# Seven products instead of eight for half of the row pairs of a 256x8192x2048 product in fp32, with its stationaries sent to DRAM and read back

## The chip, the cores and the metric

The kernel runs on one core of a Trainium2 chip. The metric is device time in microseconds (us) of one execution; lower is better. Engines are named as in the profile: PE is the matrix engine (PEld its weight loads), DVE, ACT and POOL are the vector, scalar and general engines, SP issues most of the DMAs.

## The reference, cut to what matters

One encoder layer on 256 tokens of 2048 features: a mixer of two attention branches, then a squared-ReLU MLP. The change touches only the MLP, and in it the down projection:

```python
h = rms_norm(x, norm_mlp_pre)
u = square(relu(h @ w_up))           # [256, 2048] @ [2048, 8192]
x = x + rms_norm(u @ w_down, norm_mlp_post)   # [256, 8192] @ [8192, 2048], all fp32
```

## The kernel before

Every fp32 product is made of parts. A weight block of 1 MB is loaded by SP into a `raw` buffer (`load`, L98), ACT casts it into `hi` (L115), DVE subtracts to get `lo` (L116). `raw`, `hi` and `lo` have three buffers each (pool `wp`, `bufs=3`), so SP's load of block n+3 waits until DVE's subtraction of block n has freed the `raw` buffer. SP works through its DMAs in order: what stands behind a waiting load waits too.

Up projection (the loop over 16 groups `cg` of 512 columns, 4 weight blocks each): weights are stationary, the transposed normalised input is moving (`wgroup`, L191 and L192). Each of a group's four banks `u_p` is taken out by ACT (`up_r`, L254), DVE (`up_s`, L256 and L761) and ACT (`u`, L762). The 16 results `u` [128, 4, 256] stay in SBUF as pages, transposed: 512 rows of the down projection by 256 tokens.

Down projection (L769 to L819): activations are stationary, `w_down` is moving. `usplit` (L746, L747) makes the parts `uh`, `ul` of a group of four 128-row blocks. A step k takes one block of 128 rows and all 2048 columns: two token tiles `t`, four column blocks `c` of 512, and for each of these eight accumulators `acc` three matmuls of 128x128 by 128x512 (L777, L778, L779: `uh` with `hi`, `uh` with `lo`, `ul` with `hi`), 24 a step, 64 steps, 1536 in all. The eight accumulators fill all eight PSUM banks. The last three steps (`LAST = 3`) go accumulator by accumulator, token tile 0 first, so that most of the evacuation runs under the products that are left. Evacuation of an accumulator is a square with a sum on ACT (`jd`, L807) and a multiplication by the gain on DVE (`zw`, L809). Per token tile then follow the mean and the inverse root (`sd`, `rd`, L811 and L85 on DVE, L88 on POOL), four times scale-and-add of the residual on DVE (L816), and four stores (L819).

The program order on every engine is set when the program is built, by a list scheduler with a cost model; code order only breaks ties, except where `issue_after` pins an instruction. On the chip each engine takes its instructions in that order.

## Time and profile before

| | |
|---|---|
| three runs | 1395.98, 1396.07, 1398.43 us, median 1396.07 us |
| profiled execution | span 1394.5 us; its own device time is not given apart, the median lies 1.6 us above the span |
| PE busy | 1374.6 us (99%) |
| DVE, ACT, POOL busy | 835.8 us (60%), 668.7 us (48%), 7.9 us (1%) |
| DMA | 265.16 MB, mean 190 GB/s |

The profile page gives the busy time of each engine over the whole span and in 40 slices, the DMA queues, the chain of work that ended last, and the costliest groups of instructions. An engine counts as busy while it has an instruction in work; matmuls overlap, so the time between the starts of two of them is shorter than the 389 ns that one is given. The first step of a reading is which engine the chain runs through, and the second whether the others have room in the stage that is changed.

### The profile page before, as it was taken

To read this page: it belongs to the slowest core of one execution; us is meant where nothing else is said; L and a number is where in the kernel's file an instruction comes from. 1 tells how busy PE (TensorE), PEld (TensorE's weight loads), DVE (VectorE), ACT (ScalarE), POOL (GpSimd) and SP (SyncE) were. 2 spreads that over 40 slices of the span, in tenths; PEclk is the share of its full clock that TensorE was granted. 3 is DMA by queue.
4 is the path that set the end of the run, shared out by engine and by line. 5 is a ranking of instruction groups with operands and counts; after the bars stand their busy time and mean duration, and the time that the engine had idled before them with its cause. 6 is when DMAs were issued, how large, how long until landed. Compare 5 with 4: busy or idle time off the path is not lost.

```text
span 1394.5 us, 17896 instructions
## 1 busy us (share of the span) xinstructions
PE 1374.6 (99%) x7240; PEld 1177.8 (84%) x7240; DVE 835.8 (60%) x1155; ACT 668.7 (48%) x1023; POOL 7.9 (1%) x19
## 2 busy tenths in 40 slices
PE   7999999999999999999899999999999999999997
PEld 6888888888888888888788888888888888888886
DVE  6868866676656565654755555555575554444445
ACT  7554554545444445543744444444464543334332
POOL 0000000000000000000000000000000000000000
PEclk9999999999999999999999999999999999999999
DMA  9674755564555555675455565656555556555551
GB/s 317 202 214 154 202 177 173 171 191 155 165 205 182 203 181 183 203 279 184 149 182 181 182 193 170 211 170 200 189 196 185 203 186 227 195 187 205 181 199 73
DMA packets 117490, 265.16 MB, mean 190 GB/s; under 512 B 15008, under 2 KB 16288, under 8 KB 109216
## 3 DMA queue, kind: packets, MB, share of 16 engines
q1 hardware_dynamic: 117264, 264.03, 57.3%
q8 instruction: 56, 0.92, 0.3%
q14 instruction: 26, 0.21, 0.0%
q10 hardware_dynamic: 144, 0.01, 0.0%
HBM read 261.92 MB, written 3.92 MB: 191 GB/s over the span
## 4 chain that ended last, share of the span: by engine, by line
PE 98%; DVE 1%; DMA 0%; ACT 0%; SPq 0%; issue 0%; DVEq 0%; POOLq 0%; POOL 0%; ACTq 0%
PE u_p L191 17%; PE u_p L192 9%; PE acc L779 8%; PE acc L778 8%; PE acc L777 8%; PE gb_p L191 4%; PE ga_p L191 4%; PE qa_p L191 2%; PE gb_p L192 2%; PE ga_p L192 2%; PE ka_p L191 2%; PE qn_p L191 2%; PE bb_p L191 2%; PE ba_p L191 2%; PE kn_p L191 2%; PE y_p L229 2%
## 5 line engine op out<-in xcount | busy, mean ns | idle before, releaser
L191 PE MATMUL u_p<-h2T,u_h 128*128 128x512 f32 x1024 | 359.9, 398 | 0.5 <-DVE r_m L85 0.5
L192 PE MATMUL u_p<-h2T,u_l 128*128 128x256 f32 x1024 | 284.3, 280 | 0.0
L116 DVE TENSOR_TENSOR d_l<-d_w,d_h 128x1024 fp32r<-128x1024 f32 x128 | 151.1, 1221 | 164.2 <-ACT d_h L115 163.7
L116 DVE TENSOR_TENSOR u_l<-u_w,u_h 128x1024 fp32r<-128x1024 f32 x128 | 151.1, 1222 | 146.0 <-ACT u_h L115 144.7
L191 PEld LDWEIGHTS u_p<-h2T,u_h 128*128 128x128 f32 x1024 | 192.0, 189 | 45.5 <-DVE r_m L85 0.9
L115 ACT CAST d_h<-d_w 128x1024 fp32r<-128x1024 f32 x128 | 128.3, 1052 | 191.1 <-PE acc L779 187.5
L778 PE MATMUL acc<-d_l,uh 128*128 128x512 f32 x512 | 199.0, 389 | 0.0
L779 PE MATMUL acc<-d_h,ul 128*128 128x512 f32 x512 | 198.9, 389 | 0.0
L777 PE MATMUL acc<-d_h,uh 128*128 128x512 f32 x512 | 198.2, 389 | 0.0
L192 PEld LDWEIGHTS u_p<-h2T,u_l 128*128 128x128 f32 x1024 | 193.8, 189 | 1.3
L115 ACT CAST u_h<-u_w 128x1024 fp32r<-128x1024 f32 x128 | 128.0, 1049 | 123.9 <-PE u_p L191 62.5
L778 PEld LDWEIGHTS acc<-d_l,uh 128*128 128x128 f32 x512 | 96.1, 188 | 20.1
L777 PEld LDWEIGHTS acc<-d_h,uh 128*128 128x128 f32 x512 | 96.1, 188 | 20.0
L779 PEld LDWEIGHTS acc<-d_h,ul 128*128 128x128 f32 x512 | 96.1, 188 | 19.8
L191 PE MATMUL gb_p<-hT,gb_h 128*128 128x512 f32 x256 | 90.4, 398 | 0.0
L191 PE MATMUL ga_p<-hT,ga_h 128*128 128x512 f32 x256 | 90.0, 397 | 0.0
L192 PE MATMUL gb_p<-hT,gb_l 128*128 128x256 f32 x256 | 71.4, 281 | 0.0
L192 PE MATMUL ga_p<-hT,ga_l 128*128 128x256 f32 x256 | 70.3, 280 | 0.0
L191 PEld LDWEIGHTS gb_p<-hT,gb_h 128*128 128x128 f32 x256 | 47.9, 188 | 11.5
L116 DVE TENSOR_TENSOR gb_l<-gb_w,gb_h 128x1024 fp32r<-128x1024 f32 x32 | 37.8, 1221 | 31.1 <-ACT gb_h L115 31.1
L191 PEld LDWEIGHTS ga_p<-hT,ga_h 128*128 128x128 f32 x256 | 47.4, 188 | 10.5
L116 DVE TENSOR_TENSOR y_l<-y_w,y_h 128x1024 fp32r<-128x1024 f32 x32 | 37.9, 1222 | 27.8 <-ACT y_h L115 27.8
(213 smaller groups left out, 2348.1 us busy)
## 6 DMA issues: line engine op xcount, KB each, us to landing
u_w<-in_w_up SPq DMA_DIRECT2D x64, 1024.0 KB, 5.4
d_w<-in_w_down SPq DMA_DIRECT2D x64, 1024.0 KB, 4.9
ga_w<-in_w_in SPq DMA_DIRECT2D x16, 1024.0 KB, 5.2
gb_w<-in_w_in SPq DMA_DIRECT2D x16, 1024.0 KB, 5.2
y_w<-in_w_out SPq DMA_DIRECT2D x16, 1024.0 KB, 5.1
ka_w<-in_w_in SPq DMA_DIRECT2D x8, 1024.0 KB, 6.1
va_w<-in_w_in SPq DMA_DIRECT2D x8, 1024.0 KB, 5.2
qn_w<-in_w_in SPq DMA_DIRECT2D x8, 1024.0 KB, 5.1
```

Source lines behind the costliest of these rows:

```text
L115: nc.scalar.copy(hi[part], raw[part])
L116: nc.vector.tensor_sub(lo[part], raw[part], hi[part].bitcast(F32))
L191: nc.tensor.matmul(ps[b], hi[:, k % 4, cs], mv, start=(k == 0), stop=False)
L192: nc.tensor.matmul(ps[b][:, :T], lo[:, k % 4, cs], mv[:, :T], start=False, stop=(k == nk - 1))
L229: nc.tensor.matmul(ps[t], sh, hi[:, k % 4], start=(k == 0), stop=False)
L777: nc.tensor.matmul(acc[t][c], uh[:, k % 4, ts_], hi[:, 0, cs], start=(k == 0), stop=False)
L778: nc.tensor.matmul(acc[t][c], uh[:, k % 4, ts_], lo[:, 0, cs], start=False, stop=False)
L779: nc.tensor.matmul(acc[t][c], ul[:, k % 4, ts_], hi[:, 0, cs], start=False, stop=(k == NK - 1))
```

## The change

A step of the new down projection takes two blocks of 128 rows (a row pair) and half of the columns (1024, `g` = 0 or 1), again 1 MB of `w_down`. It is a product of 2x2 blocks: two token tiles by two row blocks, two row blocks by two column blocks of 512. For odd groups `cg` ("eight") it is done as before, eight block products, 24 matmuls. For even ones ("seven") it is done with seven products of sums of blocks, 21 matmuls: four sums of activation blocks are made once (`sums`, on DVE), four sums of weight blocks in each step (`dt`, on DVE), and the products are put together from eight banks `p{g}0` to `p{g}7` when all row pairs of the half are summed (`zw`, on DVE). There are 32 steps of either kind; the matmuls go from 1536 to 1440.

All steps of `g = 0` come before those of `g = 1`, so each stationary is used twice, in times far apart. Stationaries are made behind each group of the up projection (`act_sets`: `ah`, `al`), written to DRAM by POOL (`keep`), and read back by SP, for each `g` anew (`act_again`: `bh`, `bl`), two groups ahead of their use. The pool `tmp` is closed behind the up projection, and its room goes to the parts `eh`, `el` of the weight sums, with one buffer each. `dr`, `dh`, `dl` are the weight block as loaded and its two parts, with three buffers each as before.

```diff
+    temps = ctx.enter_context(ExitStack())
+    tmp = temps.enter_context(tc.tile_pool(name="tmp", bufs=6))
...
+    NG = DFF // 512
+    kept = {}
+    def seven_of(cg):
+        return cg % 2 == 0
+    def act_sets(cg, u):
+        srcs = []
+        if seven_of(cg):
+            a11, a21 = u[:, 0:2, :P], u[:, 0:2, P:]
+            a12, a22 = u[:, 2:4, :P], u[:, 2:4, P:]
+            sums = page([P, 4, 2, P], F32, f"sm{cg}")
+            nc.vector.tensor_sub(sums[:, 0], a21, a22)
+            nc.vector.tensor_sub(sums[:, 1], a11, a21)
+            nc.vector.tensor_sub(sums[:, 2], sums[:, 0], a11)
+            nc.vector.tensor_add(sums[:, 3], a12, sums[:, 2])
+            srcs = [
+                ([P, 3, 2, P], [(slice(0, 1), u[:, 0:2, :P].unsqueeze(1)),
+                                (slice(1, 3), u[:, 2:4].rearrange("p k (t q) -> p t k q", t=2))]),
+                ([P, 4, 2, P], [(slice(0, 4), sums)]),
+            ]
+        else:
+            srcs = [([P, 4, T], [(slice(0, 4), u)])]
+        for i, (shape, pieces) in enumerate(srcs):
+            hi, lo = page(shape, F32R, f"ah{cg}{i}"), page(shape, F32R, f"al{cg}{i}")
+            for at, src in pieces:
+                nc.scalar.copy(hi[:, at], src)
+                nc.vector.tensor_sub(lo[:, at], src, hi[:, at].bitcast(F32))
+            for n, part in (("h", hi), ("l", lo)):
+                kd = dram.tile(shape, F32, name=f"keep{n}{cg}{i}", tag=f"keep{n}{cg}{i}")
+                nc.gpsimd.dma_start(kd, part.bitcast(F32))
+                kept[cg, i, n] = (shape, kd)
+    def act_again(cg, g):
+        out = []
+        for i in range(2 if seven_of(cg) else 1):
+            got = []
+            for n in "hl":
+                shape, kd = kept[cg, i, n]
+                t = page(shape, F32R, f"b{n}{g}{cg}{i}")
+                nc.sync.dma_start(t.bitcast(F32), kd)
+                got.append(t)
+            out.append(got)
+        return out
+    for cg in range(NG):
         u = page([P, 4, T], F32, f"u{cg}")
 
         def u_evac(b, ps, u=u):
@@ -762,57 +799,139 @@
             nc.scalar.activation(u[:, b], s, AF.Square)
 
         wgroup(a["w_up"], cg * 512, lambda k: hT2[k // 2][:, k % 2], KD, u_evac, f"u{cg}", **({} if cg else first_up))
-        uT.append(u)
-        if cg == DFF // 512 - 2:
-            usplit(0)
-
...
+        act_sets(cg, u)
+    temps.close()
+    down = ctx.enter_context(tc.tile_pool(name="down", bufs=1, reuse_waits="tile"))
+    wd = a["w_down"].rearrange("(g h j p) c -> p h g j c", h=2, j=2, p=P)
+    def wtile(tag, name):
+        return wp.tile([P, 4, 512], F32R, tag=tag, name=name)
+    def down_weights(g, cg, j):
+        raw = wp.tile([P, 4, 512], F32, tag="raw", name=f"dr{g}{cg}{j}")
+        last_load[0] = nc.sync.dma_start(
+            raw.rearrange("p (h b) c -> p h (b c)", h=2),
+            wd[:, :, cg, j, g * 1024 : (g + 1) * 1024],
+        ).ins
+        n = f"{g}{cg}{j}"
+        h1, l1 = wtile("hi", f"dh{n}"), wtile("lo", f"dl{n}")
+        if not seven_of(cg):
+            nc.scalar.copy(h1, raw)
+            nc.vector.tensor_sub(l1, raw, h1.bitcast(F32))
+            return h1, l1
+        t = [page([P, 2, 512], F32, f"dt{n}{i}") for i in range(2)]
+        nc.scalar.copy(h1[:, 1:4], raw[:, 1:4])
+        nc.vector.tensor_add(t[0], raw[:, 1:3], raw[:, 0:1].to_broadcast([P, 2, 512]))
+        nc.vector.tensor_add(t[1][:, 0], t[0][:, 0], raw[:, 2])
+        nc.vector.tensor_add(t[1][:, 1], t[1][:, 0], raw[:, 3])
+        nc.vector.tensor_sub(l1[:, 1:4], raw[:, 1:4], h1[:, 1:4].bitcast(F32))
+        h2 = down.tile([P, 4, 512], F32R, tag="h2", name=f"eh{n}")
+        l2 = down.tile([P, 4, 512], F32R, tag="l2", name=f"el{n}")
+        for i in range(2):
+            at = slice(i * 2, i * 2 + 2)
+            nc.scalar.copy(h2[:, at], t[i])
+            nc.vector.tensor_sub(l2[:, at], t[i], h2[:, at].bitcast(F32))
+        return h1, l1, h2, l2
+    class Products:
+        def __init__(self, name, low):
+            self.ps = [bank(f"{name}{i}", i in low) for i in range(8)]
+            self.begun = set()
+        def add(self, i, stat, w, blk, last=False):
+            (sh, sl), (wh, wl) = stat, w
+            nc.tensor.matmul(self.ps[i], sh, wh[:, blk], start=i not in self.begun, stop=False)
+            self.begun.add(i)
+            nc.tensor.matmul(self.ps[i], sh, wl[:, blk], start=False, stop=False)
+            nc.tensor.matmul(self.ps[i], sl, wh[:, blk], start=False, stop=last)
+    def seven(pr, sets, j, w, last):
+        def stat(i, at):
+            return tuple(part[:, at, j] for part in sets[i])
+        r, t = w[:2], w[2:]
+        pr.add(0, stat(0, 0), r, 1, last)
+        pr.add(4, stat(1, 0), t, 0, last)
+        pr.add(6, stat(1, 1), t, 1, last)
+        pr.add(5, stat(1, 2), t, 2, last)
+        pr.add(2, stat(1, 3), r, 2)
+        pr.add(1, stat(0, 1), r, 3)
+        pr.add(3, stat(0, 2), t, 3)
+    PLAIN = ((1, 0, 1), (2, 0, 0), (3, 1, 1), (7, 1, 0))
+    def eight(pr, sets, j, w, which, last):
+        i, t, half = PLAIN[which]
+        for k in (0, 2):
+            stat = tuple(part[:, j + k, t * P : (t + 1) * P] for part in sets[0])
+            pr.add(i, stat, w, k + half, last and k == 2)
 
     gp2 = [page([P, 1024], F32, f"gp2{h}") for h in range(2)]
     for h in range(2):
         nc.sync.dma_start(
             gp2[h], a["g_mlp_post"][:, h * 1024 : (h + 1) * 1024].partition_broadcast(P)
         )
-    ws = [dweight(k) for k in range(NK - LAST, NK)]
+    sets = {(0, cg): act_again(cg, 0) for cg in range(2)}
+    zw = {}
+    ssd = [small(4, f"ssd{t}") for t in range(2)]
+    for g in range(2):
+        steps = []
+        for b in range(0, NG, 2):
+            s0, s1, n0, n1 = (b, 0), (b, 1), (b + 1, 0), (b + 1, 1)
+            if g == 0:
+                steps += [n0, s0, n1, s1] if b < NG - 2 else [n0, s0, s1, n1]
+            else:
+                steps += [s0, n0, s1, n1]
+        pr = Products(f"p{g}", (0, 4, 5, 6))
+        for i, (cg, j) in enumerate(steps):
+            end = i == len(steps) - 1
+            w = down_weights(g, cg, j)
+            if i % 4 < 2:
+                nxt = (g, i // 4 * 2 + 2 + i % 4)
+                if nxt[1] >= NG:
+                    nxt = (g + 1, nxt[1] - NG)
+                if nxt[0] < 2:
+                    with tc.issue_after(last_load[0]):
+                        sets[nxt] = act_again(nxt[1], nxt[0])
+            if seven_of(cg):
+                final = not any(seven_of(c) for c, _ in steps[i + 1 :])
+                seven(pr, sets[g, cg], j, w, final)
+                if final:
+                    for t in range(2):
+                        zw[g, t] = page([P, 2, 512], F32, f"zw{g}{t}")
+                    c11, c12 = zw[g, 0][:, 1], zw[g, 0][:, 0]
+                    c21, c22 = zw[g, 1][:, 1], zw[g, 1][:, 0]
+                    nc.scalar.copy(c11, pr.ps[0])
+                    nc.vector.tensor_add(c12, c11, pr.ps[5])
+                    nc.vector.tensor_add(c21, c12, pr.ps[6])
+                    nc.vector.tensor_sub(c12, pr.ps[4], c12)
+                    nc.vector.tensor_sub(c22, pr.ps[4], c21)
+                continue
+            for which in range(4):
+                eight(pr, sets[g, cg], j, w, which, end)
+                if end:
+                    i_, t, half = PLAIN[which]
+                    z = zw[g, t][:, half]
+                    nc.vector.tensor_add(z, z, pr.ps[i_])
+                    sq = down.tile([P, 512], F32, tag="junk", name=f"jd{g}{which}", bufs=2)
+                    c = g * 2 + half
+                    nc.scalar.activation(sq, z, AF.Square, accum_out=ssd[t][:, c : c + 1])
+                    nc.vector.tensor_mul(z, z, gp2[g][:, half * 512 : (half + 1) * 512])
     for t in range(2):
...
-        nc.vector.tensor_reduce(sd, ssd, axis=AX.X, op=ALU.add)
+        nc.vector.tensor_reduce(sd, ssd[t], axis=AX.X, op=ALU.add)
         rd = inv_rms(sd, D, f"rd{t}")
         for c in range(4):
             cs = slice((c % 2) * 512, (c % 2 + 1) * 512)
-            z = zw[c // 2][:, cs]
+            z = zw[c // 2, t][:, c % 2]
             nc.vector.scalar_tensor_tensor(
                 z, z, rd, x2[t * 2 + c // 2][:, cs], op0=ALU.mult, op1=ALU.add
             )
```

The line numbers of code that is kept go up by one at L98 and by more behind it (L116 to L117, L256 to L257).

PE's rows are the same up to the last matmul of the up projection, and there are 96 fewer behind it. SP at the seam between the up and the down projection, before (`u15_3_w` is the last weight block of the up projection, `d*_w` the blocks of the down projection):

```order
L98 DMA u15_3_w_9142<-in_w_up 128x4x512
L98 DMA d0_w_9214<-in_w_down 128x2048
L98 DMA d1_w_9222<-in_w_down 128x2048
L98 DMA d2_w_9278<-in_w_down 128x2048
L98 DMA d3_w_9310<-in_w_down 128x2048
L98 DMA d4_w_9346<-in_w_down 128x2048
```

and after (`dr` weight blocks, `gp2` the gain, `bh`/`bl` stationaries):

```order
L814 DMA dr000_9518<-in_w_down 128x2x1024
L814 DMA dr011_9560<-in_w_down 128x2x1024
L814 DMA dr001_9590<-in_w_down 128x2x1024
L814 DMA dr030_9628<-in_w_down 128x2x1024
L877 DMA gp20_9454<-in_g_mlp_post 128x1024
L877 DMA gp21_9455<-in_g_mlp_post 128x1024
L788 DMA bh000_9458<-keeph00_6378 128x768
L788 DMA bl000_9460<-keepl00_6380 128x768
L788 DMA bh001_9462<-keeph01_6386 128x1024
L788 DMA bl001_9464<-keepl01_6388 128x1024
L788 DMA bh010_9466<-keeph10_6583 128x1024
L788 DMA bl010_9468<-keepl10_6585 128x1024
```

In place of weight loads alone stand five weight loads, the two loads of the gain, and the read-back of the first stationaries, all on the one queue. The name `dr030` is half 0, group 3, j 0, and so on; two weight loads, `dr010` and `dr000`, stand ahead of these rows.

DVE at the same seam, before:

```order
L256 TENSOR_TENSOR up_s_9188<-u15_p2_9020,up_r_9186 128x256
L761 SCALAR_TENSOR_TENSOR up_s_9188<-up_s_9188,r2b_5461 128x256
L747 TENSOR_TENSOR ul1_9343<-u1_6367,uh1_9342 128x1024
L116 TENSOR_TENSOR d2_l_9281<-d2_w_9278,d2_h_9280 128x1024 x2
L256 TENSOR_TENSOR up_s_9202<-u15_p3_9021,up_r_9200 128x256
L747 TENSOR_TENSOR ul2_9475<-u2_6556,uh2_9474 128x1024
L761 SCALAR_TENSOR_TENSOR up_s_9202<-up_s_9202,r2b_5461 128x256
L747 TENSOR_TENSOR ul3_9607<-u3_6745,uh3_9606 128x1024
L747 TENSOR_TENSOR ul4_9739<-u4_6934,uh4_9738 128x1024
```

and after (`al15` is the last stationary made, `dt` are sums of weight blocks, `el` their lo part):

```order
L822 TENSOR_TENSOR dl011_9563<-dr011_9560,dh011_9562 128x2048
L257 TENSOR_TENSOR up_s_9438<-u15_p3_9257,up_r_9436 128x256
L798 SCALAR_TENSOR_TENSOR up_s_9438<-up_s_9438,r2b_5461 128x256
L774 TENSOR_TENSOR al150_9443<-u15_9253,ah150_9442 128x1024
L827 TENSOR_TENSOR dt0000_9522<-dr000_9518 128x1024
L828 TENSOR_TENSOR dt0001_9523<-dt0000_9522,dr000_9518 128x512
L827 TENSOR_TENSOR dt0010_9594<-dr001_9590 128x1024
L829 TENSOR_TENSOR dt0001_9523<-dt0001_9523,dr000_9518 128x512
L836 TENSOR_TENSOR el000_9530<-dt0000_9522,eh000_9529 128x1024
L828 TENSOR_TENSOR dt0011_9595<-dt0010_9594,dr001_9590 128x512
L836 TENSOR_TENSOR el000_9530<-dt0001_9523,eh000_9529 128x1024
```

Behind the last evacuation of the up projection (`u15_p3`) there was a subtraction per weight block; now a subtraction of 2048 stands ahead of it and the stationary, five sums and the two halves of `el000` behind it.

DVE at the seam between the two halves of the columns, which the kernel before does not have (`p0*` are the banks of the first half, `dr1*` weight blocks of the second):

```order
L923 TENSOR_TENSOR zw00_10634<-zw00_10634,p01_9473 128x512
L827 TENSOR_TENSOR dt1000_10699<-dr100_10695 128x1024
L915 TENSOR_TENSOR zw00_10634<-p04_9476,zw00_10634 128x512
L916 TENSOR_TENSOR zw01_10635<-p04_9476,zw01_10635 128x512
L830 TENSOR_TENSOR dl101_10778<-dr101_10775,dh101_10777 128x1536
L927 TENSOR_TENSOR zw00_10634<-zw00_10634,gp20_9454 128x512
L828 TENSOR_TENSOR dt1001_10700<-dt1000_10699,dr100_10695 128x512
L923 TENSOR_TENSOR zw00_10634<-zw00_10634,p02_9474 128x512
L836 TENSOR_TENSOR el100_10707<-dt1000_10699,eh100_10706 128x1024
L923 TENSOR_TENSOR zw01_10635<-zw01_10635,p03_9475 128x512
L923 TENSOR_TENSOR zw01_10635<-zw01_10635,p07_9479 128x512
L827 TENSOR_TENSOR dt1010_10779<-dr101_10775 128x1024
```

The work on the results of the first half lies between the weight work of the second, and the banks that it reads are the ones that the second half writes next.

DVE at the end, before (`acc1*` are the accumulators of token tile 1):

```order
L816 SCALAR_TENSOR_TENSOR zw00_11255<-zw00_11255,rd0_r_11309,x2_0_5443 128x512 x2
L816 SCALAR_TENSOR_TENSOR zw01_11256<-zw01_11256,rd0_r_11309,x2_1_5444 128x512 x2
L809 TENSOR_TENSOR zw10_11320<-acc11_9211,gp20_11226 128x512
L809 TENSOR_TENSOR zw11_11321<-acc12_9212,gp21_11227 128x512
L809 TENSOR_TENSOR zw11_11321<-acc13_9213,gp21_11227 128x512
L811 TENSOR_REDUCE sd1_11370<-ssd1_11319 128x1
L85 TENSOR_SCALAR rd1_m_11372<-sd1_11370 128x1
L816 SCALAR_TENSOR_TENSOR zw10_11320<-zw10_11320,rd1_r_11374,x2_2_5445 128x512 x2
L816 SCALAR_TENSOR_TENSOR zw11_11321<-zw11_11321,rd1_r_11374,x2_3_5446 128x512 x2
```

and after (`p1*` are the eight banks of the second half of the columns):

```order
L916 TENSOR_TENSOR zw11_11838<-p14_10691,zw11_11838 128x512
L923 TENSOR_TENSOR zw10_11837<-zw10_11837,p12_10689 128x512
L927 TENSOR_TENSOR zw10_11837<-zw10_11837,gp21_9455 128x512
L923 TENSOR_TENSOR zw11_11838<-zw11_11838,p13_10690 128x512
L923 TENSOR_TENSOR zw11_11838<-zw11_11838,p17_10694 128x512
L927 TENSOR_TENSOR zw10_11837<-zw10_11837,gp21_9455 128x512
L930 TENSOR_REDUCE sd0_11890<-ssd0_9470 128x1
L927 TENSOR_TENSOR zw11_11838<-zw11_11838,gp21_9455 128x512
L86 TENSOR_SCALAR rd0_m_11892<-sd0_11890 128x1
L927 TENSOR_TENSOR zw11_11838<-zw11_11838,gp21_9455 128x512
L930 TENSOR_REDUCE sd1_11904<-ssd1_9471 128x1
L935 SCALAR_TENSOR_TENSOR zw00_10634<-zw00_10634,rd0_r_11894,x2_0_5443 128x512 x2
```

Token tile 0 was multiplied, scaled and stored while products of tile 1 were left; now the sums of both token tiles stand behind one another (four more of them ahead of these rows), and the scale-and-adds behind these (six more follow).

More of the change, by code (lines that the diff above doesn't have):

```diff
@@ L45, in encoder_layer @@
     wp = ctx.enter_context(tc.tile_pool(name="wp", bufs=3))
-    tmp = ctx.enter_context(tc.tile_pool(name="tmp", bufs=6))
     tiny = ctx.enter_context(tc.tile_pool(name="tiny", bufs=8))
     dram = ctx.enter_context(tc.tile_pool(name="dram", bufs=1, space=bass.MemoryType.DRAM))
+    temps = ctx.enter_context(ExitStack())
+    tmp = temps.enter_context(tc.tile_pool(name="tmp", bufs=6))
     mm = ctx.enter_context(tc.tile_pool(name="mm", bufs=NMM, space=PSUM))
@@ L740, in encoder_layer @@
     )
-    ust = {}
-    def usplit(i):
-        uh = page([P, 4, T], F32R, f"uh{i}")
-        ul = page([P, 4, T], F32R, f"ul{i}")
-        nc.scalar.copy(uh, uT[i])
-        nc.vector.tensor_sub(ul, uT[i], uh.bitcast(F32))
-        ust[i] = (uh, ul)
-    def dweight(k):
-        if k % 4 == 0 and k // 4 not in ust:
-            usplit(k // 4)
-        return weight(a["w_down"], k, 1, 0, D, f"d{k}")
-    uT = []
-    for cg in range(DFF // 512):
+    NG = DFF // 512
[40 more added lines that the diff above has]
+    for cg in range(NG):
         u = page([P, 4, T], F32, f"u{cg}")
@@ L764, in encoder_layer @@
         wgroup(a["w_up"], cg * 512, lambda k: hT2[k // 2][:, k % 2], KD, u_evac, f"u{cg}", **({} if cg else first_up))
-        uT.append(u)
-        if cg == DFF // 512 - 2:
-            usplit(0)
-    acc = [[bank(f"acc{t}{c}", t * 4 + c >= 8 - NMM) for c in range(4)] for t in range(2)]
-    NK = DFF // P
-    LAST = 3
-    def dmm(k, t, c, w):
-        uh, ul = ust[k // 4]
-        ts_ = slice(t * P, (t + 1) * P)
-        cs = slice(c * 512, (c + 1) * 512)
-        hi, lo = w
-        nc.tensor.matmul(acc[t][c], uh[:, k % 4, ts_], hi[:, 0, cs], start=(k == 0), stop=False)
-        nc.tensor.matmul(acc[t][c], uh[:, k % 4, ts_], lo[:, 0, cs], start=False, stop=False)
-        nc.tensor.matmul(
-            acc[t][c], ul[:, k % 4, ts_], hi[:, 0, cs], start=False, stop=(k == NK - 1)
-        )
@@ L783, in encoder_layer @@
-    ws = [dweight(k) for k in range(2)]
-    for t in range(2):
-        for k in range(2):
-            for c in range(4):
-                dmm(k, t, c, ws[k])
-    for k in range(2, NK - LAST):
-        w = dweight(k)
-        for t in range(2):
-            for c in range(4):
-                dmm(k, t, c, w)
+        act_sets(cg, u)
+    temps.close()
+    down = ctx.enter_context(tc.tile_pool(name="down", bufs=1, reuse_waits="tile"))
+    wd = a["w_down"].rearrange("(g h j p) c -> p h g j c", h=2, j=2, p=P)
@@ L798, in encoder_layer @@
         )
-    ws = [dweight(k) for k in range(NK - LAST, NK)]
-    for t in range(2):
-        ssd = small(4, f"ssd{t}")
-        zw = [page([P, 1024], F32, f"zw{t}{h}") for h in range(2)]
-        for c in range(4):
-            for i in range(LAST):
-                dmm(NK - LAST + i, t, c, ws[i])
-            j = junk512("jd").rearrange("p a b -> p (a b)")
-            nc.scalar.activation(j, acc[t][c], AF.Square, accum_out=ssd[:, c : c + 1])
-            cs = slice((c % 2) * 512, (c % 2 + 1) * 512)
-            nc.vector.tensor_mul(zw[c // 2][:, cs], acc[t][c], gp2[c // 2][:, cs])
+    sets = {(0, cg): act_again(cg, 0) for cg in range(2)}
```

## The prediction

> **What bounds the kernel now.** I read the page first, for the chain and the busy shares, then the groups by line, then the stage that is changed by itself.
>
> ```profile
> span 1394.5 us, 17896 instructions
> PE 1374.6 (99%) x7240; PEld 1177.8 (84%) x7240; DVE 835.8 (60%) x1155; ACT 668.7 (48%) x1023; POOL 7.9 (1%) x19
> PE   7999999999999999999899999999999999999997
> PEclk9999999999999999999999999999999999999999
> PE 98%; DVE 1%; DMA 0%; ACT 0%; SPq 0%; issue 0%; DVEq 0%; POOLq 0%; POOL 0%; ACTq 0%
> ```
>
> The chain runs through PE for 98% of the span, and PE is full in all slices but the first and the last. So taking matmuls away shortens the time one for one, and any gap that the change opens on PE is added whole. The price of a matmul in the down projection comes from the tile view of the accumulators (count, shortest/median/longest ns, first and last start), the room beside it from the windows (length, then busy time of PE, PEld, DVE, ACT and POOL, clock, DMA share, GB/s): the up projection's second half, the down projection, and the two places where the DMA queues were full.
>
> ```profile
> L777 PE MATMUL acc<-d_h,uh x512: 389/389/398, 1037.2 to 1384.7; 128*128 128x512 f32 x171
> L779 PE MATMUL acc<-d_h,ul x512: 388/389/395, 1037.7 to 1385.2; 128*128 128x512 f32 x171
> 680.00:1037.00 357.00, 357.00 (x2049) 311.42 (x2048) 202.58 (x276) 176.11 (x278) 0.54 (x1) 1.00 0.59 189
> 1037.00:1385.00 348.00, 348.00 (x1538) 288.13 (x1537) 172.51 (x155) 144.05 (x157) 0.54 (x1) 1.00 0.54 187
> 8.00:20.00 12.00, 10.80 (x56) 9.37 (x56) 9.09 (x15) 11.90 (x27) 0.00 (x0) 1.00 1.04 388
> 592.00:598.00 6.00, 6.00 (x28) 4.96 (x27) 2.36 (x2) 2.43 (x3) 0.00 (x0) 1.00 1.02 413
> ```
>
> From the first start at 1037.2 to the last at 1385.2 there are 1535 steps of one matmul: 348.0 / 1535 = 226.7 ns each, at the full clock (1.00). A step of 24 takes 5.44 us. DVE and ACT are busy for half of the stage (172.5 and 144.1 of 348 us), and the DMA moves 187 GB/s where it has been seen to move about 400.
>
> **The change part by part.** *Fewer matmuls.* 32 steps lose three each: 96 x 226.7 ns = **-21.8 us**. The shapes are the same, so the price holds.
>
> *The work beside PE in the steady state* is taken from these groups (busy us, mean ns, idle before) and the weight loads of the page (us to landing).
>
> ```profile
> L116 DVE TENSOR_TENSOR d_l<-d_w,d_h 128x1024 fp32r<-128x1024 f32 x128 | 151.1, 1221 | 164.2 <-ACT d_h L115 163.7
> L115 ACT CAST d_h<-d_w 128x1024 fp32r<-128x1024 f32 x128 | 128.3, 1052 | 191.1 <-PE acc L779 187.5
> L809 DVE TENSOR_TENSOR zw<-acc,gp 128x512 f32<-128x512 f32 x8 | 5.3, 688 | 6.2 <-ACT jd L807 5.9
> u_w<-in_w_up SPq DMA_DIRECT2D x64, 1024.0 KB, 5.4
> d_w<-in_w_down SPq DMA_DIRECT2D x64, 1024.0 KB, 4.9
> ```
>
> DVE's time grows by (1221 - 688) / 512 = 1.04 ns an element: 1.75 us for 1536, 2.28 for 2048. A seven step costs DVE 1.22 + 2 x 0.69 + 1.75 + 2 x 1.22 = 6.8 us, an eight step 2.28, the pair 9.1 us. The pair takes PE 45 x 0.2267 = 10.2 us. ACT needs some 5.5. Loads per pair are 2.10 MB of weights and 1.44 MB of stationaries, 3.54 MB or 347 GB/s, against the 388 and 413 GB/s of the full queues: 8.6 to 9.1 us. So PE stays the bound, but DVE and the queue go from half full to 85 to 90%: 0, with a bad end at +10 for waits that add up.
>
> *The up projection* gets the sums and parts of the stationaries and 23 MB of writes. DVE had 154 us free of 357 there, and the added work over the whole stage is about 42 us on DVE and 25 on ACT, half of it in this window. PE hides it: 0, bad end +2.
>
> *The seam from up to down.* In order of time from the timeline (start, length), around the last up matmul, which ends at about 1037.2 (call it U), and the groups of the last evacuations:
>
> ```profile
> 1037.93 1.99 ACT L115 CAST d_h<-d_w 128x1024 fp32r<-128x1024 f32 x2
> 1039.00 2.36 DVE L116 TENSOR_TENSOR d_l<-d_w,d_h 128x1024 fp32r<-128x1024 f32 x2
> L256 DVE TENSOR_TENSOR up_s<-u_p,up_r 128x256 f32<-128x256 f32 x64 | 25.4, 419 | 0.0
> L762 ACT ACTIVATE u<-up_s 128x256 f32<-128x256 f32 x64 | 25.0, 418 | 25.2 <-DVE up_s L761 25.2
> SPq L98 <- DVE d_l L116: 288.2, 58, 9.1
> ```
>
> The third weight block's `lo` is done at U + 4.2, because its `hi` buffer is the one that the last up matmuls read. The last row (total us, times, longest) is SP waiting for that subtraction to free a `raw` buffer; in before nothing but the next load stands behind it. After the change the fifth load, `dr030`, waits for `dl011` in the same way, until about U + 4.4, and in SP's order both gain loads and every stationary of the first block stand behind it. PE can do only 13 of its products ahead of the first that needs `bh010`. Bytes on the queue up to and with `bh010`: 1.05 (`dr030`) + 1.05 (gains) + 0.79 + 1.05 + 0.52 = 4.46 MB, 11.1 us at 0.40 MB/us. A lone 1 MB load lands in 4.9 us, of which 2.6 are its bytes, so 2.3 are latency. `bh010` lands at U + 4.4 + 11.1 + 2.3 = U + 17.8; PE has used 13 x 0.227 = 2.9 us by then: a gap of **+14.9 us**. A second chain, independent of the first, gives nearly as much: `dl011`, the last `up_s` (0.42 twice), `u` (0.42), the stationary's cast and subtraction (1.05, 1.22), `dt0000` and the two short sums with `dt0010` between (1.22, 0.69, 1.22, 0.69), then `el000` twice, end at U + 15 or so, which holds PE's 11th product; the gap would be about 13. So ends 13 and 17, and putting right one alone would not remove it.
>
> *The clock behind that gap.* PE has one idle time in before, at the start, and the starts there show what the clock does:
>
> ```profile
> 10.21 0.63 PE L191 MATMUL qa_p<-hT,qa_h 128*128 128x512 f32 x1
> 10.64 0.41 PE L192 MATMUL qa_p<-hT,qa_l 128*128 128x256 f32 x1
> 10.85 0.63 PE L191 MATMUL qa_p<-hT,qa_h 128*128 128x512 f32 x1
> ...
> 15.12 0.40 PE L191 MATMUL qa_p<-hT,qa_h 128*128 128x512 f32 x1
> 15.36 0.28 PE L192 MATMUL qa_p<-hT,qa_l 128*128 128x256 f32 x1
> 15.48 0.40 PE L191 MATMUL qa_p<-hT,qa_h 128*128 128x512 f32 x1
> ```
>
> A pair takes 0.64 us at first and 0.36 later; the slow part runs from 9.4 to about 13, so it costs at most 1.8 us. Part of it would fall on the 13 products that are waiting anyway: **+1.0 us**, ends 0 and 1.8. The Trainium skill's TensorE: Matmul & The Clock Gate (Part 1: The HAM clock gate) says that one idle window of about 3.4 us puts the array back to half clock and that as long a busy stretch lifts it; by that the gap costs an estimated 1.7 us, and the trace's start agrees, while no gap of this length in the middle of a run is in it.
>
> *The seam between the halves.* Let V be the end of the last product of `g = 0`. DVE's rows from the first sum of results (which can start at V - 1.8, eight products earlier) to `dl120` are 16 of 512, 5 of 1024, 2 of 1536 and 1 of 2048: 16 x 0.69 + 5 x 1.22 + 2 x 1.75 + 2.28 = 22.9 us, with about 1.5 us of waits for ACT's casts and squares between them: V + 22.6. In the new order PE's first product that needs `dl120` has 74 of the second half ahead of it, 16.8 us, and they hang on banks that these same rows set free: **+5.9 us**. The good end is 4 (DVE ahead by what the waits are), the bad one 10 (each wait shown to PE on its own).
>
> *The end.* In before, from the timeline:
>
> ```profile
> 1385.18 0.39 PE L779 MATMUL acc<-d_h,ul 128*128 128x512 f32 x1
> 1385.66 0.60 ACT L807 ACTIVATE jd<-acc 128x512 f32<-128x512 f32 x1 [1.41 <-PE acc L779]
> 1386.38 0.69 DVE L809 TENSOR_TENSOR zw<-acc,gp 128x512 f32<-128x512 f32 x1 [1.41 <-ACT jd L807]
> 1387.47 0.54 POOL L88 TENSOR_TENSOR rd_r<-rd_m,expo 128x1 f32<-128x1 f32 x1 [6.69 <-DVE rd_m L85]
> 1388.05 2.74 DVE L816 SCALAR_TENSOR_TENSOR zw<-zw,rd_r,x 128x512 f32<-128x512 f32 x4 [0.72 <-POOL rd_r L88]
> ```
>
> The last product ends at 1385.6 (W), the last scale-and-add at 1390.8 (W + 5.2), the span at 1394.5: 3.7 us for the last store. After the change DVE has behind W eleven or twelve sums and gain products of 512 (12 x 0.69 = 8.3, less those that fit ahead of W), the small ones with POOL's power (0.6) and eight scale-and-adds (5.5) where there were four. That ends at about W + 13.9: **+8.6 us**, ends 7 and 10.
>
> The sum: -21.8 + 14.9 + 1.0 + 5.9 + 8.6 = **+8.6 us**. Against the profiled execution this is a span of 1403.1; the median of the runs lies 1.6 above the span of before, so 1404.7, rounded to **1405 us**.
>
> **The rivals.** *The seam is short, and the kernel faster.* The price of the first seam hangs on SP standing at `dr030`. If the stationaries of the first block land while PE still has products, and DVE's chain is not in PE's way, that term is 2 to 3 and not 14.9 + 1.0: 1396.1 - 21.8 + 2.5 + 5.9 + 8.6 = 1391. It decides from where the gap is under 7.3 us (21.8 - 5.9 - 8.6). Against it speaks the order, in which no stationary can be asked for ahead of U + 4.4. Chance 8%.
>
> *The gaps are half as long, and it comes out even.* PE has other products that it can take, DVE's waits are shorter than I count, the tail overlaps: 9 + 0 + 3 + 8 - 21.8 = -1.8, 1394, and from there up to 1399; for it speaks that waits which I add one behind another can overlap. Chance 12%.
>
> *Another bound in the steady state.* DVE at 9.1 of 10.2 us and the queue at 8.6 to 9.1 have little room; with three `raw` buffers and one buffer for `eh` and `el`, which is cast anew only when PE has read the last, a pair may take 10.7 instead of 10.2: 31 pairs x 0.5 = +15 us, 1420. For it speaks that SP's loads are lined up behind stationaries; against it that each block of steps has its stationaries asked for some 20 us (90 products) early, and that SP stood waiting for a free buffer 288 of 348 us in before, not for the queue. Chance 15%.
>
> *That it does not do what it says* can be excluded for the count: PE's rows are 96 fewer.
>
> **How the numbers follow.** 65% for the forecast, whose own range by the ends is 1399 to 1412 (-21.8 plus 13 + 0 + 4 + 7 and 17 + 1.8 + 10 + 10, narrowed since not all ends fall together), 15, 12 and 8% for the rivals. The range of 8 in 10 reaches to the even case and most of the way to the second bound: 1397 to 1418. No change is told apart from one under 0.2%, 2.8 us: faster ends at 1393.3, slower begins at 1398.9. Faster: the first rival, 8%, and a little of the second, 10% together. Same: 10%. Slower: 80%.
>
> **What would show it.** In the profile after: PE idle for about 15 us just behind the last up matmul, with `bh010` or `el000` as what ends it, some 6 us more in short waits where the banks `p1` begin, no idle time to speak of in between (a window over steps of one half should show 10.2 us a pair and a DMA rate near 350 GB/s), and 17.5 us between the last product and the end. It is wrong if PE waits in every pair, if the first block's stationaries land ahead of U + 10, or if the tail is under 14 us.

## The result and the profile after

The changed kernel takes **1408.88 us** (median, 1407.76 to 1410.30) against 1396.93 us (1395.98 to 1398.43) for the kernel before on the same chip: ratio 1.0083, 95% interval 1.0071 to 1.0094, so 12 us slower. The profiled execution has a span of 1408.1 us, 13.6 above the 1394.5 of before; its own time was 1409.97 us, 1.1 above the median. Medians and ratios below are of undisturbed runs: in 'gains_late' two of the four, the profiled one among them, took 1954 us (granted clock 0.65) and 2768 us and are left out.

From the page: span, busy time, and three of the rows of 40 slices.

```profile
span 1408.1 us, 18191 instructions
PE 1358.9 (96%) x7144; PEld 1161.9 (83%) x7144; DVE 990.2 (70%) x1315; ACT 719.8 (51%) x1041; POOL 34.4 (2%) x67
PE   7999999999999999999899999999959999999995
PEclk9999999999999999999999999999988999999998
DMA  8674655564555555676477767777779999798972
PE 95%; DVE 2%; DMA 1%; ACT 1%; issue 0%; SPq 0%; POOL 0%; DVEq 0%; POOLq 0%; ACTq 0%
```

PE is busy for 15.7 us less than before, and the span is longer. PE's row has a 5 near three quarters of the span, with a fall of the clock under it, and a 5 at the end. The last row is the chain: DVE, DMA and ACT have 4% of it now, where DVE had 1%.

What PE waited for behind the up projection (total us, times, longest):

```profile
PE p L849 <- DMA bh<-keeph: 16.8, 2, 16.2
PE p L849 <- DVE zw L923: 2.0, 2, 1.4
PE p L849 <- ACT eh L835: 0.8, 1, 0.8
PE p L851 <- DVE dl L830: 0.7, 1, 0.7
PE p L852 <- DMA bl<-keepl: 0.6, 1, 0.6
```

Most of it is one wait, for a stationary that comes back from DRAM. The windows (columns as in the prediction: length, busy time of PE, PEld, DVE, ACT and POOL with the number of instructions, clock, DMA share, GB/s) place the loss: the whole stretch from the end of the last up matmul to the end of the last product, then four pieces of it.

```profile
1039.48:1391.68 352.20, 331.36 (x1440) 271.53 (x1440) 283.05 (x240) 171.71 (x140) 1.07 (x2) 0.97 0.85 316
1039.44:1070.00 30.56, 13.17 (x44) 9.85 (x44) 11.32 (x12) 7.30 (x8) 1.07 (x2) 0.66 0.84 310
1070.00:1190.00 120.00, 120.00 (x532) 99.34 (x531) 100.62 (x81) 62.16 (x49) 0.00 (x0) 1.00 0.95 352
1190.00:1250.00 60.00, 56.51 (x245) 45.37 (x244) 55.15 (x53) 32.20 (x31) 0.00 (x0) 1.00 0.80 295
1250.00:1390.00 140.00, 140.00 (x620) 115.91 (x619) 114.31 (x95) 70.08 (x54) 0.00 (x0) 1.00 0.79 300
```

The third and the fifth row are the steady state: 532 matmuls in 120 us and 620 in 140, one each 0.226 us, PE never idle, at full clock. DVE stands at 84 and 82% there, the DMA at 352 and 300 GB/s. In the second row there are 44 matmuls where 30.56 / 0.2267 = 135 had room: 20.6 us lost. In the fourth there are 20 too few: 4.5 us, and 5.2 by the difference to the whole. The first row has 1440 matmuls, worth 326.4 us, in 352.2: 25.8 us lost in all.

| us, profiled executions | before | after | difference | forecast |
|---|---|---|---|---|
| start of the span to the last up matmul's end | 1037.4 | 1039.5 | +2.1 | 0 |
| the products at 0.2267 us | 348.2 | 326.4 | -21.8 | -21.8 |
| lost at the seam from up to down | 0 | 20.6 | +20.6 | +15.9 |
| lost at the seam between the halves | 0 | 5.2 | +5.2 | +5.9 |
| last product's end to the end of the span | 8.9 | 16.4 | +7.5 | +8.6 |
| span | 1394.5 | 1408.1 | +13.6 | +8.6 |

The 2.1 us of the first line are not put down to the change: 1.6 of them stand before the first matmul of the up projection (674.0 us in before, 675.6 after), in the first 30 us, where PE did 10 matmuls less (115 and 125). With the same code there the kernels below start it between 673.4 and 675.7. The other half microsecond falls in the up projection, whose matmuls start over 362.9 us in before and 363.3 after; 'best_b' below, with the same work there, takes 362.6.

### The profile page after: what moved, and what is told of

Same layout as the page of the kernel before. It is cut to its first block, busy times and chain, and to the rows that moved or that the text cites. A ratio compares the mean times of both kernels' runs of the same rounds, so it can differ in the third digit from the quotient of the medians.

```text
span 1408.1 us, 18191 instructions
## 1 busy us (share of the span) xinstructions
PE 1358.9 (96%) x7144; PEld 1161.9 (83%) x7144; DVE 990.2 (70%) x1315; ACT 719.8 (51%) x1041; POOL 34.4 (2%) x67
## 4 chain that ended last, share of the span: by engine, by line
PE 95%; DVE 2%; DMA 1%; ACT 1%; issue 0%; SPq 0%; POOL 0%; DVEq 0%; POOLq 0%; ACTq 0%
PE u_p L192 17%; PE u_p L193 9%; PE p L849 7%; PE p L852 7%; PE p L851 7%; PE gb_p L192 4%; PE ga_p L192 4%; PE qa_p L192 2%; PE ga_p L193 2%; PE gb_p L193 2%; PE qn_p L192 2%; PE ka_p L192 2%; PE bb_p L192 2%; PE ba_p L192 2%; PE kn_p L192 2%; PE y_p L231 2%
## 5 line engine op out<-in xcount | busy, mean ns | idle before, releaser
L117 DVE TENSOR_TENSOR u_l<-u_w,u_h 128x1024 fp32r<-128x1024 f32 x128 | 151.1, 1222 | 91.3 <-ACT u_h L116 90.0
L116 ACT CAST u_h<-u_w 128x1024 fp32r<-128x1024 f32 x128 | 128.0, 1048 | 95.6 <-PE u_p L192 83.9
L849 PE MATMUL p<-dh,bh 128*128 128x512 f32 x352 | 120.8, 392 | 18.2 <-DMA bh<-keeph 16.2
L851 PE MATMUL p<-dl,bh 128*128 128x512 f32 x352 | 137.3, 390 | 0.7 <-DVE dl L830 0.7
L852 PE MATMUL p<-dh,bl 128*128 128x512 f32 x352 | 136.8, 390 | 0.6 <-DMA bl<-keepl 0.6
L835 ACT CAST eh<-dt 128x1024 fp32r<-128x1024 f32 x64 | 65.0, 1051 | 101.1 <-PE p L852 96.8
L836 DVE TENSOR_TENSOR el<-dt,eh 128x1024 fp32r<-128x1024 f32 x64 | 77.3, 1221 | 27.5 <-ACT eh L835 27.5
L849 PEld LDWEIGHTS p<-dh,bh 128*128 128x128 f32 x352 | 66.2, 188 | 33.1 <-issue 16.5
L822 DVE TENSOR_TENSOR dl<-dr,dh 128x2048 fp32r<-128x2048 f32 x32 | 73.2, 2289 | 20.4 <-ACT dh L821 20.1
L821 ACT CAST dh<-dr 128x2048 fp32r<-128x2048 f32 x32 | 61.1, 1909 | 34.7 <-DMA dr<-in_w_down 32.5
L851 PEld LDWEIGHTS p<-dl,bh 128*128 128x128 f32 x352 | 66.4, 189 | 14.9 <-DVE dl L830 1.2
L852 PEld LDWEIGHTS p<-dh,bl 128*128 128x128 f32 x352 | 66.2, 188 | 15.1 <-DMA bl<-keepl 1.3
```

The lines of the kernel that those rows point to most:

```text
L116: nc.scalar.copy(hi[part], raw[part])
L117: nc.vector.tensor_sub(lo[part], raw[part], hi[part].bitcast(F32))
L821: nc.scalar.copy(h1, raw)
L822: nc.vector.tensor_sub(l1, raw, h1.bitcast(F32))
L835: nc.scalar.copy(h2[:, at], t[i])
L836: nc.vector.tensor_sub(l2[:, at], t[i], h2[:, at].bitcast(F32))
```

## The experiments

Each is an edit of the changed kernel. The 'stretch' is the row of the windows from the end of the last up matmul to the end of the last product, less 326.4 us (348.2 for 1536 matmuls).

**The gains out of the queue's way.** The loads of `gp2` move to step 16:

```diff
...
-    for h in range(2):
-        nc.sync.dma_start(gp2[h], ...)
...
+            if g == 0 and i == 16:
+                for h in range(2):
+                    with tc.issue_after(last_load[0]):
+                        nc.sync.dma_start(gp2[h], ...)
```

> The two loads of the gain leave the queue ahead of the first stationaries and come 16 steps later; nothing else moves. Theory (queue and DVE chain hold the first seam together): the first stationary lands about 4.7 us earlier (U + 11.5 instead of U + 16.2), then DVE's chain to el000 (done at U + 14.2 in the changed kernel) holds PE's 11th product, so 4 to 6 us are won, 1403 to 1405 us. Rival (the queue alone sets the seam): as much is won and no new wait of PE for el shows behind it; rival (bytes of the gains count as any others, 2.6 us): 1406.

Measured: 1410.08 and 1411.16 us, ratio 1.0093 (1.0073 to 1.0113), without a profile that can be compared. Neither the theory nor its rivals forecast a time above 1406. The same edit was run again.

> The same edit as gains_late (the two loads of the gain come 16 steps later), since its profile came from an execution at a granted clock of 0.65 and two of its runs lay at 1410 to 1411. Theory (the gains stand in the queue ahead of the first stationaries and they land some 4 us earlier without them): 1403 to 1406 us, and the first wait of PE behind the up projection is 10 to 12 us instead of 16.2. Rival (what is won at the seam is lost again where the gains now stand between the weight loads, or to DVE's chain): 1408 to 1411, with new waits of PE in the steady state or at the seam.

Measured: 1411.24 us, ratio 1.0101 (1.0086 to 1.0116); 2.4 us above the changed kernel, with intervals that overlap, so nothing is won. The rival holds, though the theory's first half does too. The waits of PE, and the piece of the second seam as above:

```profile
PE p L849 <- DMA bh<-keeph: 12.2, 2, 10.5
PE p L849 <- ACT dh L821: 1.6, 1, 1.6
PE p L849 <- ACT dh L826: 1.6, 1, 1.6
1190.00:1250.00 60.00, 55.14 (x223) 43.73 (x223) 52.50 (x51) 29.97 (x30) 0.00 (x0) 0.94 0.80 296
```

The first stationary lands 5.7 us earlier (PE waits 10.5 us instead of 16.2). The ones behind it win less: the fifth, `bh010`, lands 11.5 us after it is asked for at 1045.79, where it took 13.8 us from 1047.41 in the changed kernel; counted from the last up matmul's end that is 3.4 us earlier. So the gains' 1.05 MB held up the row of loads by 3.4 us, where their bytes make 2.6 at 0.40 MB/us. What makes the difference between 3.4 and 5.7 was not tried apart. POOL's writes of the last stationaries, 1.05 MB on the same engines from 1045.7 on, run beside both: the queues fell to 147 to 198 GB/s for some 2.4 us in the changed kernel, and to 246 to 317 at the same place without the gains.

PE gains 3.5 us at the first seam (61 matmuls by 1070 where it had 44, less the 0.5 us by which the up projection ended earlier), and loses 22 matmuls, 5.0 us, at the other. There two of the squares on the results (`jd`) now stand on ACT ahead of the cast of the next weight block:

```order
L928 ACTIVATE jd02_10674,ssd1_9469<-zw01_10635 128x512
L928 ACTIVATE jd03_10684,ssd1_9469<-zw01_10635 128x512
L821 CAST dh111_10815<-dr111_10813 128x2048
```

In the changed kernel the cast came first. The scheduler laid the order anew some 100 us behind the loads' new place (1120.7 us), and PE waited for that cast (1.6 us) and then ran at half clock. Of the 5.0 us only 1.3 are longer waits (4.8 us in sum instead of 3.5); some 3.3 are matmuls at half clock behind two of them.

**The first block's stationaries stay in SBUF.** The first half begins with groups 12 and 13:

```diff
+    PAIRS = ([6, 0, 1, 2, 3, 4, 5, 7], list(range(8)))
...
+            held.setdefault(cg, []).append([hi, lo])
...
-    sets = {(0, cg): act_again(cg, 0) for cg in range(2)}
+    sets = {(0, cg): held[cg] for cg in (12, 13)}
...
```

> The first block of steps uses groups 12 and 13, whose stationaries are still in SBUF, and does not read them back; the other pairs follow in their order. Theory (two chains): the wait for the read-back of 16 us goes, PE starts at U with the eight steps (48 products, 10.9 us), then DVE's chain to the lo part of the first weight sums (U + 15 to 19 in this order) shows as a gap of 4 to 8 us: won 10 to 14 us, 1395 to 1399 us. Rival (the queue alone): the gap goes wholly and the clock stays up, 20 us won, 1389. Rival (DVE alone): little won, 1405 or more.

Measured: 1395.84 us, 0.9991 (0.9982 to 1.0000). The stretch loses 13.0 us instead of 25.8: some 5 at the first seam and 7 at the second, which is 2 more there than in the changed kernel. The wait for the DMA is gone, and behind the eight steps stands DVE's chain:

```profile
1036.58:1375.99 339.41, 333.16 (x1441) 270.52 (x1439) 283.34 (x240) 171.70 (x140) 1.06 (x2) 0.99 0.84 320
1050.00:1060.00 10.00, 7.46 (x26) 5.04 (x25) 7.39 (x10) 3.05 (x3) 0.00 (x0) 0.83 1.03 418
1053.08 0.69 PE L854 MATMUL p<-el,ah 128*128 128x512 f32 x1 [2.38 <-DVE el L839]
```

The last row, from the timeline (start, length, in brackets the idle time before it), is 16.5 us behind the last up matmul. From 1050 to 1060 us there are 26 matmuls instead of 45, so 4.3 us are lost there, with a granted clock of 0.83. So a second chain, DVE's, stood behind the first, as the theory said.

**Plain steps first.** Also both eight steps of that block ahead of both seven steps:

```diff
+                if len(steps) == 4:
+                    steps = [n0, n1, s0, s1]
```

> As the one before, and in the first block both eight steps are written ahead of both seven steps, so the weight sums are needed 5.4 us later. Theory (two chains): the gap that DVE leaves shrinks to 0 to 4 us, 1391 to 1395 us. Rival (queue alone): no difference to the one before.

Measured: **1388.20 us**, 0.9933 (0.9918 to 0.9948), below the range. The stretch loses 4.9 us, of which the first seam has about one (41 matmuls instead of 45 in those 10 us):

```profile
1039.48:1370.81 331.33, 327.90 (x1441) 269.57 (x1439) 282.84 (x242) 171.66 (x142) 1.06 (x2) 1.00 0.87 327
1057.01 0.50 PE L854 MATMUL p<-el,ah 128*128 128x512 f32 x1 [0.71 <-DVE el L839]
```

The wait for the lo part of the weight sums is 0.71 us where it was 2.38, and the clock stays up. The theory was about this seam, and it explains half of what was won: of the 8 us that the stretch is shorter than in 'resident', 3.6 lie at the second seam (250 matmuls from 1190 to 1250 us instead of 234), which the edit does not name. The order came out otherwise there: on ACT three squares on results stand ahead of a weight cast in 'resident' (1216.91 to 1219.75), and one here. That part is luck.

**A warm array.** 64 matmuls on data in SBUF, into a bank that is started anew later:

```diff
...
+            with tc.issue_after(up_end[0]):
+                for _ in range(64):
+                    warm = nc.tensor.matmul(pr.ps[7], hT2[0][:, 0, :P], hT2[0][:, 0], start=True, stop=True).ins
...
```

The products of the first four steps are pinned behind these 64.

> 64 matmuls of 128x512 on operands that are in SBUF anyway run right behind the last up matmul, into a bank that is started anew afterwards; 14.5 us, less than the wait of 16.2. Theory (of the 20.4 us lost at the first seam 3 are the half clock behind the idle time): 2 to 3 us won, 1406 to 1407, with starts 0.23 us apart from the first product on. Rival (the clock costs nothing beyond the waits): no change, 1409.

Measured: 1408.14 us, 1.0075 (1.0058 to 1.0092); the stretch takes 351.7 us with the 64 in it, 0.5 less. The time is the rival's, but not for its reason. The granted clock stayed at 1.00 through the 64 and the first products behind them, and fell to 0.50 at about 1058.0, 5.5 us behind the end of the last of the 64:

```profile
1053.78 0.47 PE L850 MATMUL p<-dh,bh 128*128 128x512 f32 x1 [1.33 <-DMA bh<-keeph]
1055.62 0.50 PE L853 MATMUL p<-dh,bl 128*128 128x512 f32 x1 [1.14 <-DMA bl<-keepl]
1057.26 1.03 PE L850 MATMUL p<-eh,bh 128*128 128x512 f32 x3 [1.14 <-DMA bh<-keeph]
1058.08 1.48 PE L852 MATMUL p<-el,bh 128*128 128x512 f32 x3
```

The stationaries land piece by piece, PE starts four matmuls in the 5 us up to 1057.3, and a little later three take 1.28 us (1058.08 to the next at 1059.36), 0.43 each, the half rate. So the clock was lost all the same, at a later place. What the clock costs with the stationaries present is left open.

**The end.** The last eight step's matmuls are put behind the last seven step's:

```diff
...
-                eight(pr, sets[g, cg], j, w, which, end)
+                with tc.issue_after(pr.end) if end and g in (1,) else nullcontext():
+                    eight(pr, sets[g, cg], j, w, which, end)
```

> In the second half of the columns alone, the last eight step's 24 matmuls are put behind the last seven step's 21 on PE, one result block behind the other. Theory (16.4 us between the last product and the end because the sums of results stand behind it on DVE): four to six of the twelve sums and gain products move ahead of the last product, the stretch shrinks to 11 to 14 us, 1404 to 1406.5 us. Rival (PE then waits for the weight sums that the other order hid): as much is lost ahead of the last product, 1408 to 1410.

Measured: 1405.62 us, 1.0062 (1.0047 to 1.0077). From the end of the last product (1390.6) to the end of the span (1403.1) are 12.5 us where there were 16.4, and the stretch loses 26.6, 0.8 more. As the theory said.

```profile
1390.25 0.39 PE L852 MATMUL p<-dh,bl 128*128 128x512 f32 x1
1392.93 2.73 DVE L936 SCALAR_TENSOR_TENSOR zw<-zw,rd_r,x 128x512 f32<-128x512 f32 x4
1396.45 2.74 DVE L936 SCALAR_TENSOR_TENSOR zw<-zw,rd_r,x 128x512 f32<-128x512 f32 x4 [0.72 <-POOL rd_r L89]
```

In the changed kernel the first four scale-and-adds began 6.2 us behind the last product (1397.88 and 1391.68), here 2.3.

**Where DVE becomes the bound.** Three groups of four by seven products:

```diff
-        return cg % 2 == 0
+        return cg % 4 != 3
```

> Three of four groups use seven products instead of two of four: 48 matmuls less, 10.9 us of PE. Theory (DVE is at nearly 90% in the steady state and becomes the bound): three seven steps and one eight step cost DVE 3 x 6.8 + 2.3 = 22.7 us and PE 87 x 0.227 = 19.7 us, 16 such sets, so 48 us more by DVE and 10.9 less by PE: 1440 to 1450 us, and PE waits for el and dl in every set. Rival (PE stays the bound): 1398.

Measured: 1443.61 us, 1.0332 (1.0311 to 1.0352), in the theory's range; the waits are spread over the whole stage, and all but one (3.7 us, for a stationary) are on what DVE and ACT make:

```profile
PE p L849 <- ACT eh L835: 14.3, 24, 1.6
PE p L849 <- ACT dh L826: 9.6, 10, 2.6
PE p L851 <- DVE el L836: 8.4, 12, 2.9
```

From 1290 to 1420 us DVE is busy for 92% and ACT for 52%, and PE starts 490 matmuls, so a set of 87 takes 23.1 us, where the theory has 22.7 by DVE's work and 19.7 by PE's. `eh`, the first of the waits, is ACT's cast of the sums `dt`, which DVE makes.

**Seven products alone.** All pairs by eight, with all the rest of the variant 'best_b' below:

```diff
-        return cg % 2 == 0
+        return False
...
-                    nc.vector.tensor_add(z, z, pr.ps[i_])
+                    nc.scalar.copy(z, pr.ps[i_])
...
```

> All row pairs by eight products (1536 matmuls as in the kernel before), with all the rest of best_b: half of the columns at a time, stationaries through DRAM but for the first block, no weight sums and no recombination. Theory (seven products are worth 96 x 226.7 ns = 21.8 us of PE while PE is the bound, and the round trip through DRAM costs nothing in the steady state): 348 us between the last up matmul and the last product plus 0 to 2, an end of 10 to 12, so 1397 to 1401 us, 15 to 19 above best_b, the rest being the end that gets shorter. Rival (the round trip itself costs PE time): over 1403. Rival (much of the 21.8 is lost to DVE waits in the steady state): under 1394.

Measured: 1399.53 us, 1.0018 (1.0008 to 1.0027); 14.7 above best_b, a little under the 15 to 19 expected.

```profile
1038.28:1386.47 348.19, 348.19 (x1537) 288.00 (x1535) 148.66 (x75) 129.54 (x89) 1.33 (x3) 1.00 0.75 278
```

1536 products in 348.19 us, the same as in the kernel before to two digits: the round trip through DRAM, at 278 GB/s, costs PE nothing. Its 2 us above before are the end (11.4 us instead of 8.9), where both token tiles now end together. Against it best_b has a stretch of 332.3 us (1037.16 to 1369.48), so 15.9 of the 21.8 us arrive.

**Putting it together.** 'both' is the plain-steps-first kernel with the pin in both halves, 'best_b' adds eight steps first in the second half and moves the four gain products of the first half behind the second's first eight steps, 'best_c' moves those products alone, 'best_d' is best_b with the pin in the second half only.

> resident_plain with the last eight step pinned behind the last seven step in both halves. Theory: the first seam as in resident_plain (4.9 us lost between the last up matmul and the last product, both seams together), the end 3 to 5 us shorter: 1383.5 to 1386 us. Rival (the pin costs PE at the seam between the halves what it gives at the end): 1387 to 1390.

> The kernel both, with two edits at the seam between the halves: the second half begins with its two eight steps, and the four gain products on the results of the first half are moved behind its first eight steps. Theory (DVE's backlog of 23 us is what PE waits for there): 4 x 0.69 us and the weight sums go out of the way, 2 to 4 us won, 1381.5 to 1384 us. Rival (the wait is for banks set free by the sums of results, which stay): 1385 to 1386.

> The kernel both with the four gain products alone moved; the second half begins as before. Theory (every DVE instruction at the seam counts): 1 to 3 us won, 1382.5 to 1384.5. Rival (they were not in PE's way): 1385.5.

> best_b without the pin at the end of the first half (kept at the end of the second). Theory (the pin makes PE wait some 2 us at the end of the first half, 8 to 9 matmuls are missing from that stretch of 10 us in both and best_b and none in resident_plain; at the end of the second half it wins 4 us): 1381.5 to 1384 us, about 2 below both and best_b. Rival (without the pin the sums of results come later and the second seam waits that much longer): 1384.5 to 1386.

Measured: both 1385.51 us (0.9917, 0.9900 to 0.9934); best_b 1384.80 (0.9911, 0.9896 to 0.9926); best_c 1385.82 (0.9916, 0.9901 to 0.9930); best_d **1383.71** (0.9906, 0.9889 to 0.9922). The first is as expected. The moved gain products brought nothing that these runs can tell: for best_c the rival stands, and best_b lies between the theory's range and the rival's, with an interval that takes in both. best_d lies in its range; its interval overlaps that of best_b, so the times do not tell the two apart, but its stretch shows the pin:

```profile
1037.58:1367.86 330.28, 327.80 (x1440) 269.33 (x1438) 287.41 (x248) 173.55 (x147) 1.07 (x2) 1.00 0.88 328
1190.00:1200.00 10.00, 10.00 (x46) 8.29 (x45) 8.33 (x5) 6.54 (x6) 0.00 (x0) 1.00 0.71 247
```

3.9 us lost in the stretch against 5.9 in best_b and 6.4 in both, and the 10 us at the end of the first half are full again (46 matmuls, in both and best_b 37). It beats the kernel before by 13.6 us and the changed one by 25.

## Why the prediction was right

The direction and the range held (1405 forecast, 1397 to 1418; 1408.9 measured), and each of the terms was found at its place. That the sum came so near is in part luck: the first seam with its clock was 4.7 us dearer than forecast, and the second seam and the end were 1.8 cheaper.

**The products.** -21.8 us by the spacing of 226.7 ns; the spacing held, and the 1536 products of 'eights' against the 1440 give it again (348.2 and 326.4).

**The steady state.** Costed at nothing with DVE and the queue at 85 to 90%: PE was never idle in 260 us of it, DVE at 82 to 84%, the queue at up to 352 GB/s. The rival in which a pair takes 10.7 us did not come; 'three' shows how near it was: 16 more seven steps make DVE the bound, and the kernel 35 us slower.

**From up to down: the term that was mis-sized**, 15.9 forecast with the clock and 20.6 found. How it begins was right: SP stood until U + 4.2 at `dr030` (1043.66 us; U is the last up matmul's end, 1039.4), and the gains and the stationaries came behind it.

```profile
1043.66 0.37 SPq L814 DMA_DIRECT2D dr<-in_w_down  x1
1044.13 0.93 SPq L877 DMA_DIRECT2D gp<-in_g_mlp_post  x2
1045.15 0.62 SPq L788 DMA_DIRECT2D bh<-keeph  x1
1046.24 0.53 POOL L777 DMA_DIRECT2D keeph<-ah  x1 [19.15 <-ACT ah L773]
1047.41 0.43 SPq L788 DMA_DIRECT2D bh<-keeph  x1
1052.46 1.22 DVE L836 TENSOR_TENSOR el<-dt,eh 128x1024 fp32r<-128x1024 f32 x1
1055.63 0.77 PE L849 MATMUL p<-dh,bh 128*128 128x512 f32 x1 [16.19 <-DMA bh<-keeph]
1058.82 1.62 PE L849 MATMUL p<-eh,bh 128*128 128x512 f32 x3 [0.60 <-DMA bh<-keeph]
1062.80 0.60 PE L849 MATMUL p<-dh,bh 128*128 128x512 f32 x1
1063.70 0.40 PE L851 MATMUL p<-dl,bh 128*128 128x512 f32 x1
```

What came later than forecast is the row of stationaries. `bh010`, forecast for U + 17.8, was asked for at 1047.41 and landed 13.8 us later, at U + 21.8. The first, `bh000`, which the same sum puts at U + 12.9, landed at U + 16.1. And PE did not wait for `bh010`: its waits are for the first three stationaries it needs (16.2, 0.6 and 0.6 us), so of the 13 products that were to run ahead of `bh010` only three were done by 1058.82. That is 18.7 us lost before the clock, where I had 14.9.

The step that failed is the sum of bytes at 0.40 MB/us. The gains' 1.05 MB went in as 2.6 us, and taking them away brought 3.4 for `bh010` and 5.7 for the first stationary. The sum also left out the last stationaries' own way to DRAM (POOL's row and one more like it, another 1.05 MB on the same engines, 2.6 us by the same estimate). The 0.8 us that the gains cost beyond their bytes and these 2.6 would be 3.4 of the 4.0 us by which `bh010` was late; what POOL's writes cost was not tried apart. DVE's chain, which I had at U + 15, ended at 1053.7, U + 14.2, and was there as a second cause when the first was taken away ('resident').

**The clock.** +1.0 forecast. The granted clock falls from 1.00 to 0.50 at about 1042.8, 3.3 us behind U, and is back at about 1063.2. Behind the last wait nine matmuls run from 1058.82 to 1062.80, 0.44 us apart instead of 0.23: 1.9 us lost, a little over the end of 1.8 that I had. With the 18.7 above that makes the 20.6. The Trainium skill (TensorE: Matmul & The Clock Gate, Part 1: The HAM clock gate) gives half rate after an idle window of about 3.4 us; the trace agrees here, with its 3.3.

**Between the halves.** +5.9 forecast (the prediction's own figures give 5.8) and 5.2 found, of which 3.5 stand in four waits of 0.6 to 1.4 us on DVE and ACT. That DVE's backlog sets it is borne out only in part: DVE is busy without a break from 1226 to 1243 us, but with the gain products out of it nothing measurable came (best_c against both). What is left waits for single casts and sums (the longest in best_d, 1.6 us, for the cast `dh`), and depends on the order there.

**The end.** +8.6 forecast (8.7 by its own figures) and 7.5 found; the last scale-and-add ended 12.5 us behind the last product, where I had 13.9, since more sums fitted ahead of it.

The rival that ends on the other side had its deciding point at a first seam under 7.3 us; 'resident_plain' makes it 1 us, and is 9 us faster than the kernel before, where that rival had 5. So the rival named the right lever, and the change as written did not pull it.

## What to carry to other kernels

When PE is the bound, fewer matmuls come in one for one only where nothing starts anew: this change won 21.8 us over 330 us of steady state and gave back 33 at its two seams and its end. Look at every place where a stage begins for what has to be there first, and on which queue it is asked for behind what; work that needs nothing new (data still in SBUF, steps without sums) goes first and covers the rest. Take away both chains that meet at a seam, and after an edit compare the order in the far places too, since the scheduler lays them anew.
